# A hybrid block: each HGRN2 head's norm and gate become a task of their own, and the head's outputs use the projections' PSUM banks

## The chip, the cores and the metric

One core of one Trainium2 chip. The metric is the device time of one execution in microseconds (us), lower is better. The engines are TensorE (PE, matmuls; PEld is its weight load), VectorE (DVE), ScalarE (ACT), GpSimd (POOL) and SyncE (SP), which issues most of the DMAs. Matmul results land in PSUM, which has eight banks of 128 x 512 f32.

## What is computed

One layer on 1024 tokens of width 1024: a token-mixing part with three groups of channels, then a mixture of 16 experts. The change is in the readout of the gated linear recurrence (HGRN2), which has four heads of width 128. Cut to what matters:

```python
def hgrn2_inputs(z, lb):
    q, f_fwd, f_bwd, i, g = jnp.split(z, 5, axis=-1)
    q = heads(jax.nn.silu(q)) * (HG_HEAD_DIM ** -0.5)
    for d, f_raw in enumerate((f_fwd, f_bwd)):
        forget = lbd + (1.0 - lbd) * jax.nn.sigmoid(f_raw)
        dirs.append((heads(1.0 - forget), heads(jnp.log(forget))))

def hgrn2_bidir(q, v, dirs, s0_fwd, s0_bwd):
    s_f, o_f = gla_chunk_scan(q, k_f, v, g_f, s0_fwd)
    s_b, o_b = gla_chunk_scan(flip(q), flip(k_b), flip(v), flip(g_b), s0_bwd)
    return s_f, s_b, o_f + flip(o_b)

def hgrn2_readout(o, g, norm_g):
    on = o * lax.rsqrt(jnp.mean(o * o, axis=-1, keepdims=True) + RMS_EPS)
    return on.reshape(B, L, D_HG) * norm_g * jax.nn.silu(g)

y = jnp.concatenate([y_hy, y_hg, y_fn], axis=-1) @ w_out
```

Here o are a head's outputs, `hgrn2_readout` the norm and the gate, and the last line the out-projection, to which every head's gated output is an input.

## The kernel before

The program is written as tasks (Python generators) that a planner, `Weave`, weaves into one order. A task yields what its next piece costs (`T(us)` on PE; `V` or `B` on DVE, ACT and POOL), and the planner always lets the task run next whose piece would start first by its own clocks; among equals the lower rank goes first. `("set", x)` and `("need", x)` order tasks among themselves, and `("spawn", task, rank)` starts one. The order so written is then laid out for each engine by the compiler's scheduler, which also knows when PSUM tiles become free. On the chip each engine works through its own list in that fixed order.

PSUM is split into two pools of four banks: `psc`, from which `self.bank` takes (scores, states, norms), and `psp`, from which `self.pbank` takes (the projections `zps` and, later, the out-projection `mxps`).

In the stretch that the change touches, two tasks run side by side.

* `ins` makes the inputs of the heads (`head_in`): for each of four heads the projections k (forward), k (backward), q and g. One projection holds two of the `psp` banks and is 48 matmuls of 128 x 512 (lines 299 to 301: three products each, since operands are split into a high and a low part, `wh`/`wl`, `hx`). Then ACT and DVE take it out of PSUM. The gate g lies in a buffer of which there is one (`ptp`, `bufs=1`), so from the second head on `head_in` waits for `head{h-1}`, that the head before is done with it, before g is taken out; until then g's projection stays in its two banks. From the third head on, k needs `head{h-2}`. After the four heads comes `open_mix` and the first half of the out-projection, `mix(0)`.
* `outs` runs `fnet`, then the heads one after the other (`heads`, `head`), then `open_moe` and the second half, `mix(1)`.

`head(h)` in order: states of two directions (`kd` on DVE and ACT, `ktps` transposes on PE, `kt` out of PSUM on ACT, `ups` products on PE, `st` updates on DVE); eight levels of scores (`ee` exponentials, `scps` and `strps` products on PE), put together by masked copies (line 1424, then the last four, line 1430, into `scs`); `qd`; the outputs `ops` (lines 1448 to 1450, 24 products, each two records in the trace); the norm (`chan_rstd`, lines 868 to 909: squares `sq` on ACT, their sums `ssps` on PE line 886, twelve small DVE operations from line 584 on for the inverse root `cr`, its split `crh`/`crl`, two diagonal matrices `dg` on DVE and ACT line 897, and `rmsps` on PE line 907, which spreads the factor over the channels); the gate (lines 1460 and 1461 on DVE); and, for heads 0 to 2, a DMA of the result to `ydr`.

I call the stretch from a head's last scores to the next head's first `ups` a seam; there are seam 0 (between heads 0 and 1), 1 and 2, and seam 3 (end of the last head). A period is the time from the first `ops` of a head to the first `ops` of the next.

Of the kernel before, what the change touches and what calls it, by code (L numbers as in the profile page):

```python
# [268 lines left out]
def T(us):  # L269
    return ("pe", us)  # L270


class Kern:
# [889 lines left out]
    def hg_setup(self):  # L1163
# [8 lines left out]
        nc.vector.tensor_copy(self.lvm, m)  # L1172

    def head_in(self, heads):

        nc = self.nc
# [106 lines left out]
    def heads(self):  # L1283
        for h in range(4):
            yield ("need", f"q{h}")
            yield from self.head(h)
            yield ("set", f"head{h}")

    def head(self, h):
        nc, p = self.nc, self.hgp  # L1290
        vec = nc.vector
        hs = slice(h * P, h * P + P)
        r = self.hd[h]
# [40 lines left out]
        for d, (nm, e) in enumerate(zip(nms, (127, 0))):  # L1334
# [9 lines left out]
            for f in range(2):  # L1344
                yield T(0.35)
                ps = self.bank(name="ktps")
# [7 lines left out]
            for f in (0, 1) if d == 0 else (1, 0):  # L1354
                yield T(0.9)
                ps = self.bank(name="ups")
# [17 lines left out]
        for i, f in ((i, f) for i in range(8) for f in range(2)):  # L1374
# [26 lines left out]
            if hh != 16 and f == 0:  # L1401
                ps = self.bank(P, 256, name="strps")
            for c in range(4):
                for n in range(4):
                    a = 32 * n
                    if hh == 16:
                        o = sc[f][a : a + 32, c * P + a : c * P + a + 32]
                    else:
                        o = ps[a : a + 32, (4 * f + c) * 32 : (4 * f + c) * 32 + 32]
# [29 lines left out]
        o = []  # L1439
        yield ("wait", "sc")  # L1440
        yield ("wait", "qd")
        for f in range(2):
            yield T(2.6)
            ps = self.bank(name="ops")
            for c in range(4 * f, 4 * f + 4):
                w = ps[:, (c % 4) * P : (c % 4) * P + P]
                cs = slice(c * P, c * P + P)
                nc.tensor.matmul(w, self.v[:, c, hs], scs[:, cs], start=True, stop=False)
                nc.tensor.matmul(w, st[0][:, c], qd[0][:, cs], start=False, stop=False)
                nc.tensor.matmul(w, st[1][:, c], qd[1][:, cs], start=False, stop=True)  # L1450
            o.append(ps)
        yield ("need", f"g{h}")
        g = r["g"]

        rr = yield from self.chan_rstd(p, [o], P, eps=4 * P * EPS)
        yield V(2.4)
# [4 lines left out]
            vec.tensor_mul(y[:, c], g[:, c], o[f])  # L1461
        if h < 3:
            nc.sync.dma_start(self.ydr[2 + h], y)


    def bcast_row(self, pool, src, name):
# [610 lines left out]
def body(tc, io):  # L2077
    nc = tc.nc
    with ExitStack() as ctx:
# [112 lines left out]


        heads, fn = ExitStack(), ExitStack()
        K.hgs = [pool(f"hg{i}", "right", heads) for i in range(2)]
        K.ptp = pool("pt", "right", heads)
        K.fnp = pool("fnp", "right", fn)
# [123 lines left out]
```

## Time and profile before

| | |
|---|---|
| median of 3 runs | 1416.2 us (1414.52 to 1417.74) |
| the profiled execution's own time | 1413.68 us |
| its span in the profile | 1411.9 us |
| mean granted TensorE clock | 0.954 |
| PE busy | 1248.4 us (88%) |
| PEld busy | 953.9 us (68%) |
| DVE busy | 1080.7 us (77%) |
| ACT busy | 754.3 us (53%) |
| ops(0), first matmul | 575.96 us from the span's start |
| ops(1) | 641.13 |
| ops(2) | 709.16 |
| ops(3) | 787.60 |

Busy shares are means over the whole span, and several stages with different limits lie in it. So the table ends with four marks that cut the heads into three periods: what the change does must be read there. In the views, a "window" row gives busy microseconds and, in brackets, instructions of each engine in a stretch. A "timeline" row gives start, duration, engine, line, operation and tile, and in square brackets the engine's idle time just ahead and what ended it. Matmul records overlap, so a matmul's price is the distance from one start to the next, not its length.

### The profile page before, as it was taken

The numbers are of one execution on the slowest core, as the hardware profiler recorded it, in microseconds if no ns is written. First come the engines' busy times: TensorE is split into PE (matmuls) and PEld (weight loads), VectorE is DVE, ScalarE is ACT, GpSimd is POOL, SyncE is SP. The second block draws the span as 40 slices with busy tenths as digits, with TensorE's granted clock in tenths as the row PEclk, the third lists the DMA queues.
The fourth block names the chain that finished last, engine by engine and source line by source line (L and its number), as shares of the span: only waits on it lengthen the run. The fifth ranks groups of instructions, "written<-read, shape, count | busy, mean of one in ns | idle before, by whom it ended". The sixth has DMA issues, their size and how long they took to land. (4 is left out here: it accounts for less than half of the span.)

```text
span 1411.9 us, 21814 instructions
## 1 busy us (share of the span) xinstructions
PE 1248.4 (88%) x8032; PEld 953.9 (68%) x8032; DVE 1080.7 (77%) x1726; ACT 754.3 (53%) x1043; POOL 117.3 (8%) x131
## 2 busy tenths in 40 slices
PE   5989899999999899999889893899999998989881
PEld 1366678887566687878668772677777776767661
DVE  5567278874222589898988778899999999989965
ACT  2353122334232557666644444677877776777752
POOL 0010010100000000000000000221111012101110
PEclk9699999999999999999989996899999999999995
DMA  7944767727555420101161583899999999899944
GB/s 254 344 139 132 241 207 251 251 100 248 180 164 179 153 62 32 46 32 46 47 209 42 181 318 129 343 343 358 350 336 373 346 367 342 309 322 330 362 133 194
DMA packets 101116, 310.41 MB, mean 220 GB/s; under 512 B 16000, under 2 KB 25792, under 8 KB 100729
## 3 DMA queue, kind: packets, MB, share of 16 engines
q1 hardware_dynamic: 83208, 257.95, 50.0%
q0 software_dynamic: 15472, 48.72, 12.1%
q10 hardware_dynamic: 2304, 2.10, 0.5%
q8 instruction: 70, 1.15, 0.3%
q14 instruction: 62, 0.50, 0.1%
HBM read 274.18 MB, written 43.01 MB: 225 GB/s over the span
## 5 line engine op out<-in xcount | busy, mean ns | idle before, releaser
L293 DVE TENSOR_TENSOR wlo<-raw,whi 128x1024 fp32r<-128x1024 f32 x288 | 339.7, 1218 | 10.9 <-ACT whi L289 6.1
L289 ACT ACTIVATE whi<-raw 128x1024 fp32r<-128x1024 f32 x288 | 300.4, 1058 | 56.8 <-PE gups L301 26.6
L299 PE MATMUL gups<-whi,x 128*128 128x512 f32 x384 | 153.9, 401 | 20.4 <-ACT x L289 17.1
L299 PE MATMUL zps<-hx,wh 128*128 128x512 f32 x384 | 152.9, 398 | 1.2 <-DVE g L1231 1.2
L301 PE MATMUL zps<-hx,wl 128*128 128x512 f32 x384 | 153.0, 399 | 0.0
L300 PE MATMUL zps<-hx,wh 128*128 128x512 f32 x384 | 151.8, 395 | 0.0
L301 PE MATMUL gups<-whi,x 128*128 128x512 f32 x384 | 149.8, 396 | 2.0 <-issue 2.0
L300 PE MATMUL gups<-wlo,x 128*128 128x512 f32 x384 | 151.3, 394 | 0.0
L299 PEld LDWEIGHTS gups<-whi,x 128*128 128x128 f32 x384 | 73.0, 190 | 38.9 <-ACT x L289 20.9
L299 PE MATMUL dnps<-whi,ht 128*128 128x512 f32 x192 | 78.1, 407 | 21.6 <-ACT ht L289 21.6
L300 PEld LDWEIGHTS gups<-wlo,x 128*128 128x128 f32 x384 | 73.1, 190 | 16.9 <-issue 2.1
L300 PEld LDWEIGHTS zps<-hx,wh 128*128 128x128 f32 x384 | 72.5, 189 | 16.7 <-issue 2.9
L299 PEld LDWEIGHTS zps<-hx,wh 128*128 128x128 f32 x384 | 72.5, 189 | 16.2 <-DVE g L1231 1.7
L301 PEld LDWEIGHTS gups<-whi,x 128*128 128x128 f32 x384 | 72.7, 189 | 15.1
L301 PEld LDWEIGHTS zps<-hx,wl 128*128 128x128 f32 x384 | 72.5, 189 | 14.6 <-issue 0.4
L300 PE MATMUL dnps<-wlo,ht 128*128 128x512 f32 x192 | 75.9, 395 | 0.0
L301 PE MATMUL dnps<-whi,ht 128*128 128x512 f32 x192 | 74.9, 415 | 1.0 <-DVE ht L293 0.8
L293 DVE TENSOR_TENSOR wl<-wraw,wh 128x1024 fp32r<-128x1024 f32 x32 | 39.1, 1221 | 39.1 <-ACT wh L289 33.3
L1316 DVE TENSOR_TENSOR ee<-nm 128x1024 f32<-128x1024 f32 x56 | 67.7, 1218 | 0.6 <-PE scps L1396 0.5
L289 ACT ACTIVATE wh<-wraw 128x1024 fp32r<-128x1024 f32 x32 | 33.8, 1057 | 62.6 <-PE zps L300 27.6
L299 PE MATMUL mxps<-woh,yoh 128*128 128x512 f32 x128 | 54.4, 429 | 10.7 <-ACT yoh L289 8.3
L1860 POOL DMA_INDIRECT xg<-h2dr,ix x25 | 28.6, 1144 | 401.0 <-PE gups L301 228.3
(490 smaller groups left out, 2665.2 us busy)
## 6 DMA issues: line engine op xcount, KB each, us to landing
raw<-in_gu_dram SPq DMA_DIRECT2D x192, 512.0 KB, 7.3
raw<-in_dn_dram SPq DMA_DIRECT2D x96, 512.0 KB, 5.8
wraw<-in_win_dram SPq DMA_DIRECT2D x32, 512.0 KB, 4.1
aw<-in_ada_dram SPq DMA_DIRECT2D x32, 512.0 KB, 4.0
aws<-in_ada_dram SPq DMA_DIRECT2D x16, 512.0 KB, 7.6
tabh<-in_fwh_dram POOLq DMA_DIRECT2D x16, 512.0 KB, 5.4
tabl<-in_fwl_dram POOLq DMA_DIRECT2D x16, 512.0 KB, 7.1
xt<-in_x_dram SPq DMA_DIRECT2D x8, 512.0 KB, 4.3
```

The source lines that it names most:

```text
L289: nc.scalar.activation(hi, src, AF.Copy)
L293: nc.vector.tensor_sub(lo, src, hi)
L299: nc.tensor.matmul(out, lh, rh, start=start, stop=False)
L300: nc.tensor.matmul(out, lh, rl, start=False, stop=False)
L301: nc.tensor.matmul(out, ll, rh, start=False, stop=stop)
L1316: vec.tensor_tensor(view(ee, at, *two), view(nms[d], at, *two), view(nms[d], mid, [0, 2], blocks, [0, hh]), op=OP.subtract)
L1860: self.nc.gpsimd.indirect_dma_start(out=self.xg[g], out_offset=None, in_=self.h2dr if src is None else src, in_offset=bass.IndirectOffsetO ...
```

## The change

`ops` is taken from `self.pbank` where it was taken from `self.bank`. What followed `ops` in `head`, the norm and the gate, becomes a task `head_out`, which `head` spawns at its end with rank -8+h, ahead of the others (0 and up) among equals. The mark `head{h}` is set at the end of `head_out` and not by `heads`, and `heads` waits for `head3` at its end. The next head's task thus need not wait for the norm and gate of the one before in the planner. The operations, their sizes and the DMAs are the same.

```diff
     def heads(self):
         for h in range(4):
             yield ("need", f"q{h}")
             yield from self.head(h)
-            yield ("set", f"head{h}")
+        yield ("need", "head3")
...
         yield ("wait", "qd")
         for f in range(2):
             yield T(2.6)
-            ps = self.bank(name="ops")
+            ps = self.pbank(name="ops")
             for c in range(4 * f, 4 * f + 4):
...
             o.append(ps)
+
+        yield ("spawn", self.head_out(h, o), -8 + h)
+
+    def head_out(self, h, o):
+
+        nc, p = self.nc, self.hgp
+        vec = nc.vector
         yield ("need", f"g{h}")
-        g = r["g"]
+        g = self.hd[h]["g"]
 
         rr = yield from self.chan_rstd(p, [o], P, eps=4 * P * EPS)
...
         if h < 3:
             nc.sync.dma_start(self.ydr[2 + h], y)
+        yield ("set", f"head{h}")
```

How the lists of the engines move. First PE in seam 0, before: `strps` are the last scores of head 0, `zps` the projections for the next head, `ops` head 0's outputs.

```order
L1411 MATMUL strps<-ee 32x32 x32
L1411 MATMUL strps<-q,ks 32x32 x32
L300 MATMUL zps<-hx,wh 128x512
...
L1448 MATMUL ops<-scs,v 128x128
L1449 MATMUL ops<-qd,st_4007 128x128
L1450 MATMUL ops<-qd,st_4120 128x128
...
L886 MATMUL ssps<-onesr,sq 128x1 x4
L301 MATMUL zps<-hx,wl 128x512
L299 MATMUL zps<-hx,wh 128x512
```

The same place on PE after the change, from the last scores of head 0 to head 1's first states (`ktps`, `ups`); `lbps` is a small product of the router's setup.

```order
L301 MATMUL zps<-hx,wl 128x512
L1411 MATMUL strps<-ee 32x32 x96
L1411 MATMUL strps<-q,ks 32x32 x32
L1448 MATMUL ops<-scs,v 128x128
L1449 MATMUL ops<-qd,st_4007 128x128
L1450 MATMUL ops<-qd,st_4120 128x128
...
L886 MATMUL ssps<-onesr,sq 128x1 x8
L907 MATMUL rmsps<-dg,onesr 128x512 x4
L1349 MATMUL ktps<-ident,kd 128x128 x8
L1358 MATMUL ups<-v,kt 128x128 x8
L1577 MATMUL lbps<-rw,onesr 128x16 x8
L299 MATMUL zps<-hx,wh 128x512
```

Of the 50 projection matmuls that stood before `ops(0)` behind the same point of the list, and of the 33 between `ops(0)` and head 1's first `ups`, none is left there. In seam 1 there were 21 between the last scores and `ops` and 32 behind them, now none of either; in seam 2 there were 1 and some 13, of the out-projection, now 12 and none. Counted from one head's first `ops` to the next head's, the projection and out-projection matmuls are 171, 164 and 208 before and 192, 192 and 192 after; behind `ops(3)` 175 before and 192 after. The reason is in the pools: `ops` hold two of the four `psp` banks until the gate has read them, and the next head's g, which waits for that same gate, holds the other two.

DVE in seam 0, before: `crl` and `dg` belong to head 0's norm, `kd` and `st` to head 1's states, lines 1460 and 1461 are head 0's gate.

```order
L293 TENSOR_TENSOR crl<-cr_r,crh 128x8
L899 TENSOR_TENSOR dg<-ident,crh 128x1024
L1338 TENSOR_TENSOR kd<-nm_4044 128x1024
L1460 SCALAR_TENSOR_TENSOR z<-z,hgh,rmsps 128x512 x2
L1461 TENSOR_TENSOR z<-z,ops 128x512 x2
L1572 COPY lb<-lbps 128x16
L1338 TENSOR_TENSOR kd<-nm_4155 128x1024
L1366 SCALAR_TENSOR_TENSOR st_4713<-st_4713,eb_4679,ups 128x128
```

And after, where the gate has the lines 1467 and 1468:

```order
L293 TENSOR_TENSOR crl<-cr_r,crh 128x8
L899 TENSOR_TENSOR dg<-ident,crh 128x1024
L1338 TENSOR_TENSOR kd<-nm_4044 128x1024
L1467 SCALAR_TENSOR_TENSOR z<-z,hgh,rmsps 128x512 x2
L1468 TENSOR_TENSOR z<-z,ops 128x512 x2
L1338 TENSOR_TENSOR kd<-nm_4155 128x1024
L1366 SCALAR_TENSOR_TENSOR st_4688<-st_4688,eb_4659,ups 128x128
L1580 COPY lb<-lbps 128x16
L1366 SCALAR_TENSOR_TENSOR st_4688<-st_4688,eb_4659,ups 128x128 x6
L1231 SCALAR_TENSOR_TENSOR g<-g,zps 128x512 x2
```

Head 1's first `kd` stood ahead of head 0's gate already before, and still does; what moved on DVE is that head 1's own g now comes behind the seven updates of the first state.

## Rows read from the trace of the kernel before

**Rows 1.** The three periods in windows: busy us and instructions of each engine.
```profile
core 0: us, PE busy (x) PEld busy (x) DVE busy (x) ACT busy (x) POOL busy (x), PEclk, DMA share, GB/s
575.96:641.13 65.17, 62.35 (x785) 52.18 (x783) 60.47 (x89) 44.14 (x61) 0.00 (x0) 1.00 0.14 45
641.13:709.16 68.03, 59.26 (x760) 48.98 (x761) 61.68 (x89) 42.97 (x60) 0.00 (x0) 0.96 0.17 61
709.16:787.60 78.44, 74.22 (x805) 60.01 (x804) 66.93 (x113) 34.33 (x54) 0.00 (x0) 0.95 0.35 114
```

**Rows 2.** Two windows of 10 us, one in head 0, one in head 3.
```profile
550.00:560.00 10.00, 9.99 (x165) 7.77 (x165) 10.00 (x11) 7.25 (x9) 0.00 (x0) 1.00 0.05 9
...
740.00:750.00 10.00, 10.00 (x72) 8.14 (x70) 6.75 (x15) 1.27 (x2) 0.00 (x0) 1.00 0.18 52
```

**Rows 3.** PE's timeline in seam 0 (columns as told above).
```profile
558.34 0.39 PE L301 MATMUL zps<-hx,wl 128*128 128x512 f32 x1
...
573.23 0.39 PE L301 MATMUL zps<-hx,wl 128*128 128x512 f32 x1
...
575.72 0.40 PE L300 MATMUL zps<-hx,wh 128*128 128x512 f32 x1
575.96 0.38 PE L1448 MATMUL ops<-scs,v 128*128 128x128 f32 x2
...
583.60 0.95 PE L886 MATMUL ssps<-onesr,sq 128*128 128x1 f32 x8
...
589.07 0.85 PE L907 MATMUL rmsps<-dg,onesr 128*128 128x512 f32 x3
...
594.45 2.05 PE L1358 MATMUL ups<-v,kt 128*128 128x128 f32 x16
...
597.04 1.04 PE L1349 MATMUL ktps<-ident,kd 128*128 128x128 f32 x8
```

**Rows 4.** ACT's timeline in seam 0.
```profile
582.17 0.59 ACT L876 ACTIVATE sq<-ops 128x512 f32<-128x512 f32 x1
...
587.29 2.46 ACT L897 ACTIVATE dg<-ident,crl 128x128 fp32r<-128x128 f32 x8 [1.12 <-DVE crl L293]
...
591.05 1.06 ACT L1339 ACTIVATE kd<-kd 128x1024 f32<-128x1024 f32 x1
```

**Rows 5.** DVE's timeline in seam 0.
```profile
584.59 0.17 DVE L584 TENSOR_SCALAR cr_h<-ssps 128x8 f32<-128x8 f32 x1 [0.66 <-PE ssps L886]
...
589.96 0.75 DVE L1460 SCALAR_TENSOR_TENSOR z<-z,hgh,rmsps 128x512 f32<-128x512 f32 x1 [0.44 <-PE rmsps L907]
...
595.65 0.35 DVE L1366 SCALAR_TENSOR_TENSOR st<-st,eb,ups 128x128 f32<-128x128 f32 x1 [1.30 <-PE ups L1358]
```

**Rows 6.** PE's timeline, last scores and first outputs, in seams 1 and 3.
```profile
634.82 0.74 PE L1411 MATMUL strps<-q,ks 128*32 128x32 f32 x62
...
641.13 0.46 PE L1448 MATMUL ops<-scs,v 128*128 128x128 f32 x2 [0.57 <-DVE scs L1430]
...
783.21 0.74 PE L1411 MATMUL strps<-q,ks 128*32 128x32 f32 x62
...
787.60 0.46 PE L1448 MATMUL ops<-scs,v 128*128 128x128 f32 x2
```

**Rows 7.** PE's timeline in seam 2, from the last scores to head 3's transposes.
```profile
701.35 0.74 PE L1411 MATMUL strps<-q,ks 128*32 128x32 f32 x62
708.57 0.79 PE L299 MATMUL mxps<-woh,yoh 128*128 128x512 f32 x1 [6.48 <-ACT yoh L289]
709.16 0.63 PE L1448 MATMUL ops<-scs,v 128*128 128x128 f32 x2
...
714.28 0.42 PE L1448 MATMUL ops<-scs,v 128*128 128x128 f32 x2
...
724.46 2.09 PE L907 MATMUL rmsps<-dg,onesr 128*128 128x512 f32 x4 [0.55 <-DVE dg L899]
726.90 1.59 PE L1349 MATMUL ktps<-ident,kd 128*128 128x128 f32 x8 [0.35 <-DVE g L1460]
```

## The prediction, made before the changed kernel was run

> **What bounds the kernel now.** The page's busy shares (PE 88%, DVE 77%) mix stages, so I first cut the trace into the three periods from one head's first `ops` to the next one's [rows 1]. In the first, 65.17 us long, PE works 62.35 us and DVE 60.47: PE stands idle for 2.8 us only, DVE for 4.7. In the second PE is idle for 8.8 us, DVE for 6.3; in the third for 4.2 and 11.5. Within a period the two take turns: DVE is full in the scores of head 0 while PE is full too, and in head 3 PE stays full while DVE has a third of its time free [rows 2]. PE is full because projection matmuls fill every hole in the heads' own chains. Their pitch is 0.227 us (eleven steps from 573.23 to 575.72) [rows 3], so a projection of 48 takes 10.9 us and four of them, what a period has to hold, 43.6. In the first period 171 of them are 38.8 us; the other 23.5 us of PE's work are scores, states, outputs and norm. So PE's amount of work sets the pace in the first period, with DVE close behind, and the seams are the places where the heads' own chain alone would leave PE idle.
>
> **What the change does to PE's list.** It keeps every operation and DMA, and DVE's list hardly moves: the next head's first `kd` stood ahead of the gate before and still does, so the overlap with the next head's states that the change makes possible in the planner was there already in the list that runs. What moves is the filler. With `ops` in two of the four `psp` banks and the waiting g in the other two, no projection can be laid into the seams. The 50 matmuls ahead of `ops(0)` and the 33 behind it are gone from seam 0, the 21 and 32 from seam 1, the 13 behind `ops(2)` from seam 2. They are done later, when PE has its own work to do. I cost that period by period, each against its own length in the trace.
>
> **The chain in a seam.** From `ops` to the end of the next head's first `ups`, with nothing between: `ops` 5.5 us (575.96 to 581.5); second half of the squares 0.6 [rows 4]; their sums 0.8 and the small DVE operations 2.7 (584.59 until ACT starts on `dg` at 587.29) [rows 3 to 5]; `dg` on ACT 2.5 and the exponential of `kd` behind it 1.1 [rows 4]; transposes, their copy and `ups` 3.3 (593.2, where the transposes begin, to 596.5) [rows 3]. Together 16.5, and one us for some eight hand-overs from engine to engine, which DVE shows as waits of 0.44 to 1.30 where PE's filler came in between [rows 5]: 17.5 us. PE's own part is 5.5 for `ops`, 1.9 for `ssps`, 1.3 for `rmsps`, 1.0 for `ktps` and 2.1 for `ups` [rows 3], 11.8. So PE is idle for about **5.7 us in each seam**; I allow 1 us either way. `rmsps` and the gate run beside the exponential and the transposes and set no end here.
>
> **The masks ahead of `ops`.** After the last scores DVE still has masked copies to make before `ops` can run. PE covered that with filler. From the start of the last scores to `ops` it is 4.4 us in seam 3 (783.21 to 787.60) and 6.3 in seam 1 (634.82 to 641.13) [rows 6]; without the scores themselves, 0.7, that is 3.7 and 5.6. In seam 1 PE will be idle for all of it; I take 3.7, since in seam 1 a weight split was laid in between on DVE, and keep 3.0 and 5.6 as ends. In seam 2, 12 matmuls stay (2.7 us) and leave 1.0. In seam 0 DVE, not PE, leads up to `ops(0)` (full in that stretch [rows 2]), so I leave `ops(0)` at 576 us, cost nothing and expect PE idle instead: its last projection ahead of `ops(0)` will be the one that now starts at 558.34 [rows 3]. If DVE had slack there, `ops(0)` would come earlier, which is in the rivals.
>
> **The sum at full clock.**
> First period: 21 more matmuls, 4.8; the seam, 5.7; the masks, 3.7 less the 0.57 that PE waits there now [rows 6]: +13.6.
> Second: 192 for 164, 6.4; the seam 5.7; masks 1.0 less about 0.6; and less the 6.48 that PE now waits for the out-projection's first operands at 708.57 [rows 7], since projections stand there instead: +6.0.
> Third: 192 for 208, -3.6; the seam 5.7; masks 1.0; less the 4.2 of idle time that the period has now [rows 1] and less the 3.8 that it now pays for the lower clock (worked out below): -4.9.
> Behind `ops(3)`: 17 more, 3.9.
> Sum **18.6**.
>
> **The clock.** After 6.48 us without work PE's matmuls run at 1.2 GHz until 714.28 and at 2.4 behind it [rows 7]; the granted clock of that period is 0.95 [rows 1]. The price is read there: 12 pairs of `ops` take 5.12 us where they would take 2.68 at the later pitch, 2.4 more; `rmsps` 2.09 after a wait against some 1.2 in seam 0, where three of the four take 0.85, and `ktps` 1.59 against 1.04 [rows 3, 7], 1.4 more. Whether the clock falls in the new seams no row shows. Without any fall the cost is 0; with both in all three seams, 11.4. I take `rmsps` and `ktps` in all three (4.2), which stand behind waits just as at 724.46, and the `ops` part once, in seam 0 (2.4), where PE's list has only scores for some 16 us: **6.6**.
>
> The profiled run of 1413.7 us becomes 1413.7 + 18.6 + 6.6 = 1438.9. The median of the runs is 2.5 above that run, so 1416.2 + 25.2 = **1441 us**. The experts behind the mixing do the same work and are moved as a whole.
>
> **Rivals.**
> *DVE is the bound and PE's holes cost nothing; faster.* The place is again the seams: with no filler in front of `ssps`, `rmsps` and `ups`, DVE no longer waits for them (0.66, 0.44 and 1.30 in seam 0 [rows 5]), and the norm and the states come earlier. If DVE set the pace, the first two periods would shrink by up to DVE's idle time in them, 4.7 and 6.3 [rows 1], half of which I give to the seams or all of it: 1405 to 1411 us. It decides if PE has slack left for the displaced matmuls, at least 4.8 us in the first period. Against it: PE has 2.8 there and must lay 53 displaced matmuls (12 us) of seam 1 and 33 of seam 0 outside the seams. For it: PE's busy time is a soft measure.
> The Trainium skill says so as a rule ("Perfetto Trace Analysis", Identifying the Most-Contended Engine): busy share is a fair measure for VectorE, but for TensorE matmul busy time is not, and weight-load busy time is to be used. By that measure the first period has PE at 52.18 of 65.17 (80%) and DVE at 60.47 (93%) [rows 1], and DVE would be the engine to relieve, which gives this rival's 1405 to 1411. What speaks against the rule here is the pitch: with matmuls of 512 columns back to back the weight load is busy 7.77 of 10 us while PE takes no more work [rows 2].
> *The holes close elsewhere; nearly the same.* The change does not do what it says (the overlap was there), and the displaced matmuls fall into time in which PE waits today: 2.8, 8.8 and 4.2 us of idle in the periods [rows 1], against 51 more matmuls behind `ops(0)` (11.6 us) and the seams. If the seams are only half as long as I make them and the clock stays up, 0 to +8: 1416 to 1424 us.
> *The clock falls for whole seams; slower still.* If every `ops` runs at 1.2 GHz throughout, each head pays 4.9 (24 pairs at 0.427 instead of 0.223 [rows 7]), 19.6 for four, and `rmsps` and `ktps` 4.2: 23.8 instead of 6.6. With half to all of that excess: 1450 to 1458 us.
>
> **How the numbers follow.** Forecast (PE paces, seams are holes): 0.75. DVE the bound: 0.10. Holes close elsewhere: 0.10, of which 0.04 within 0.2% (2.8 us, about what a measurement of this kernel can tell from no change). Clock low throughout: 0.05. The forecast's own range: down by 6.6 (clock never falls), 3 (three seams a us shorter) and 0.7 (masks) to 1431; up by 4.8 (`ops` at the lower clock in two more seams), 3 and 1.9 to 1451. To hold the time 8 times in 10 the range goes down into the second rival, 1421 to 1452; what is left out is the faster rival and about half of each of the other two, 0.17. Faster 0.10, same 0.04, slower 0.86.
>
> **What would show it.** In the profile after: no `zps` between the last scores of heads 0 and 1 and the next head's first `ups`; PE idle for some 6 us in each seam behind `ops`, by waits for `sq`, `dg` and `kt`; `ops(0)` at 576, `ops(1)` near 658 (641 before), `ops(2)` near 734 (709), `ops(3)` near 808 (788); a granted clock below 1.00 in the first period. In the periods, DVE idle for more than 4.7 and 6.3 us. It is wrong if `ops(1)` comes at 641 or sooner (DVE paces), or if the seams are filled by work that I did not see; and if the seams are as said but the end moves less, then the out-projection or the experts took it back.

## The result and the profile after

The changed kernel takes 1440.1 us (median, 1437.5 to 1442.4), the kernel before 1417.0 in the runs beside it: a ratio of 1.0165 (95% interval 1.0138 to 1.0191), 20 to 27 us slower. 1441 was forecast. The profiled execution has a span of 1439.8 us (1411.9 before) and a mean granted clock of 0.942 (0.954).

First the windows, cut at the first `ops` of each head as in [rows 1], which has the columns. In the first fence the changed kernel: the stretch ahead of `ops(0)` and the three periods.

```profile
500.00:575.34 75.34, 62.70 (x745) 51.16 (x743) 70.15 (x106) 48.86 (x68) 0.00 (x0) 0.90 0.15 44
575.34:659.24 83.90, 73.34 (x804) 61.27 (x805) 63.24 (x90) 45.06 (x61) 0.00 (x0) 0.91 0.12 39
659.24:735.52 76.28, 69.09 (x788) 57.07 (x788) 56.51 (x83) 40.96 (x57) 0.00 (x0) 0.93 0.05 16
735.52:813.87 78.35, 68.21 (x789) 55.61 (x789) 68.84 (x114) 37.20 (x57) 0.00 (x0) 0.93 0.43 141
```

The same stretch ahead of `ops(0)` in the kernel before:

```profile
500.00:575.96 75.96, 72.62 (x797) 58.84 (x795) 71.18 (x108) 50.14 (x71) 0.00 (x0) 1.00 0.14 44
```

The periods are 83.9, 76.3 and 78.4 us where they were 65.2, 68.0 and 78.4 [rows 1]. PE is idle for 12.6 us ahead of `ops(0)` (3.3 before), and for 10.6, 7.2 and 10.1 in the periods (2.8, 8.8, 4.2). From `ops(3)` to the end of the span it is 625.9 us after and 624.3 before. DVE's work in the three periods is the same in sum (188.6 us, 189.1 before); its idle time grows to 20.7 and 19.8 us in the first two (4.7 and 6.3 before).

PE's timeline in seam 0 of the changed kernel, to be held against [rows 3]:

```profile
557.54 0.76 PE L1411 MATMUL strps<-ee 128*32 128x32 f32 x64
...
559.50 0.40 PE L301 MATMUL zps<-hx,wl 128*128 128x512 f32 x1
561.99 0.75 PE L1411 MATMUL strps<-ee 128*32 128x32 f32 x64 [2.09 <-DVE ee L1382]
567.99 1.08 PE L1411 MATMUL strps<-ee 128*32 128x32 f32 x64 [5.26 <-DVE ee L1382]
570.17 1.08 PE L1411 MATMUL strps<-ee 128*32 128x32 f32 x64 [1.09 <-DVE ee L1382]
...
575.34 0.79 PE L1448 MATMUL ops<-scs,v 128*128 128x128 f32 x2 [3.23 <-DVE scs L1430]
...
580.62 0.56 PE L1448 MATMUL ops<-scs,v 128*128 128x128 f32 x2
...
583.47 1.90 PE L886 MATMUL ssps<-onesr,sq 128*128 128x1 f32 x16
589.36 2.05 PE L907 MATMUL rmsps<-dg,onesr 128*128 128x512 f32 x4 [3.99 <-DVE dg L899]
591.56 1.97 PE L1349 MATMUL ktps<-ident,kd 128*128 128x128 f32 x8 [0.15 <-ACT kd L1339]
593.42 2.61 PE L1358 MATMUL ups<-v,kt 128*128 128x128 f32 x16
595.87 1.86 PE L1577 MATMUL lbps<-rw,onesr 128*128 128x16 f32 x16
597.58 0.48 PE L299 MATMUL zps<-hx,wh 128*128 128x512 f32 x1
```

The last projection matmul is the sixth behind the score level at 557.54, the same one that starts at 558.34 in [rows 3]. Then 38 us pass without one. PE waits for DVE's levels, for the masks, for `dg`, and does the first half of `ops` at the lower clock (twelve pairs in 5.3 us, from 575.34 to 580.62). Over the heads these waits add up as follows (PE's waits from 520 to 880 us: sum, times, longest):

```profile
PE rmsps L907 <- DVE dg L899: 16.4, 4, 7.0
PE strps L1411 <- DVE ee L1382: 10.7, 5, 5.3
PE ops L1448 <- DVE scs L1430: 10.5, 4, 4.6
```

### The profile page after: what moved, and what is told of

Same layout as the page of the kernel before. It is cut to its first block, busy times and chain, and to the rows that moved or that the text cites. A ratio compares the mean times of both kernels' runs of the same rounds, so it can differ in the third digit from the quotient of the medians.

```text
span 1439.8 us, 21803 instructions
## 1 busy us (share of the span) xinstructions
PE 1255.8 (87%) x8032; PEld 961.7 (67%) x8032; DVE 1081.7 (75%) x1726; ACT 755.6 (52%) x1043; POOL 115.6 (8%) x131
## 5 line engine op out<-in xcount | busy, mean ns | idle before, releaser
L299 PEld LDWEIGHTS gups<-whi,x 128*128 128x128 f32 x384 | 72.7, 189 | 34.9 <-ACT x L289 20.9
L301 PEld LDWEIGHTS gups<-whi,x 128*128 128x128 f32 x384 | 72.5, 189 | 17.9 <-issue 3.1
L300 PEld LDWEIGHTS gups<-wlo,x 128*128 128x128 f32 x384 | 72.7, 189 | 14.7
L289 ACT ACTIVATE x<-xtps 128x512 fp32r<-128x512 f32 x48 | 29.9, 624 | 55.7 <-PE xtps L1881 47.9
```

What stands on the lines that cost most here:

```text
L289: nc.scalar.activation(hi, src, AF.Copy)
L299: nc.tensor.matmul(out, lh, rh, start=start, stop=False)
L300: nc.tensor.matmul(out, lh, rl, start=False, stop=False)
L301: nc.tensor.matmul(out, ll, rh, start=False, stop=stop)
```

## The experiments

Marks (the first `ops` of each head) are from one profiled execution of each kernel, and a few us between two marks prove nothing by themselves: head 0's first transposes start at 530.5 us in after_h0 and at 534.0 in after_fill, where the code ahead of them is the same. The last column is the span behind `ops(0)`, the fifth counts the projection and out-projection matmuls behind `ops(0)` in PE's list.

| kernel | median us | ratio to before (95%) | ops(0) | matmuls behind | periods | behind ops(0) |
|---|---|---|---|---|---|---|
| before | 1413 to 1417 | | 576.0 | 718 | 65.2, 68.0, 78.4 | 835.9 |
| changed | 1440.1 | 1.0165 (1.0138 to 1.0191) | 575.3 | 768 | 83.9, 76.3, 78.4 | 864.5 |
| bank_only | 1451.0 | 1.0276 (1.0244 to 1.0308) | 574.5 | 768 | 83.3, 81.9, 81.5 | 872.7 |
| spawn_only | 1409.7 | 0.9952 (0.9932 to 0.9971) | 580.1 | 718 | 64.6, 64.1, 78.2 | 827.9 |
| after_h0 | 1427.0 | 1.0093 (1.0063 to 1.0124) | 573.8 | 768 | 83.1, 65.5, 83.2 | 851.4 |
| after_g2 | 1438.7 | 1.0178 (1.0151 to 1.0205) | 585.7 | 768 | 71.7, 72.7, 80.3 | 851.4 |
| split35 | 1437.2 | 1.0156 (1.0114 to 1.0198) | 587.8 | 768 | 77.3, 73.8, 77.3 | 848.2 |
| spawn35 | 1413.5 | 0.9991 (0.9968 to 1.0013) | 590.5 | 697 | 68.0, 66.5, 71.0 | 825.4 |
| own33 | 1422.4 | 1.0072 (1.0043 to 1.0101) | 583.7 | 707 | 61.4, 71.4, 78.3 | 833.0 |
| spawn_only_g2 | 1416.8 | 1.0027 (1.0004 to 1.0049) | 585.1 | 696 | 65.7, 58.3, 76.6 | 825.4 |
| after_fill | 1438.8 | 1.0170 (1.0137 to 1.0202) | 581.1 | 768 | 80.5, 75.9, 78.6 | 857.4 |
| after_fill2 | 1441.6 | 1.0196 (1.0166 to 1.0226) | 576.9 | 768 | 80.5, 76.0, 78.5 | 861.1 |
| before_pe | 1422.9 | 1.0064 (1.0042 to 1.0087) | 583.5 | 720 | 65.7, 69.1, 84.8 | 839.0 |
| before_dve | 1419.2 | 1.0052 (1.0030 to 1.0073) | 578.5 | 705 | 66.7, 63.5, 84.3 | 837.5 |

### The two halves of the change apart

bank_only, on the kernel before:

```diff
-            ps = self.bank(name="ops")
+            ps = self.pbank(name="ops")
```

> The kernel before with one edit: ops in the projections' banks; norm and gate stay in the head's own task. Bank theory (two psp banks for ops and two for the waiting g leave no bank for filler): its PE list has the same empty seams as the changed kernel (0, 0 and 9 projection matmuls in seam 0; none in seam 1; none in seam 2), so the whole loss: 1434 to 1444 us. Task theory (the norm and gate as a task of their own reorder the work and that is what costs): 1413 to 1421 us.

spawn_only, on the changed kernel:

```diff
-            ps = self.pbank(name="ops")
+            ps = self.bank(name="ops")
```

> The changed kernel with one edit undone: ops back in the banks of scores and states; norm and gate stay a task of their own. Bank theory: the PE list has the filler of the kernel before again (13 and 33 matmuls in seam 0, 20 and 32 in seam 1, against 13 and 33, 21 and 32), so 1413 to 1421 us, no difference that can be measured. Task theory: 1434 to 1444 us.

The bank alone costs more than the whole change: 36 us by the medians, 11 above the changed kernel (16 by the ratios) and above the range that I gave. The task alone is 0.3 to 0.7% faster than the kernel before, outside its range too, if by little, and so **faster than both kernels**. The loss is the bank's, and the task gives some of it back: 11 us or more with the bank, some 7 (4 to 10, by the interval) without.

Without the bank, the task gains 4.0 us in the second period and 3.5 in the third and the stretch behind `ops(3)` together. The second period, first of spawn_only (68.03 us before [rows 1]), then of bank_only (76.28 in the changed kernel):

```profile
644.71:708.78 64.07, 59.25 (x761) 48.61 (x761) 59.36 (x86) 40.95 (x57) 0.00 (x0) 1.00 0.09 33
```

```profile
657.79:739.72 81.93, 70.45 (x788) 58.62 (x788) 60.19 (x87) 43.59 (x60) 0.00 (x0) 0.90 0.14 44
```

spawn_only does the same 59.25 us of PE's work as before (59.26) with 4.8 us of idle time in place of 8.8. In seam 2 of its list six filler matmuls stand ahead of `ops` where one stood, and PE's wait of 6.48 us [rows 7] has gone; a wait of 3.3 us for the masks stands there. With the bank, the changed kernel's second period is 5.7 us shorter than bank_only's, and the lists show 12 matmuls ahead of `ops(2)` with the task and none without.

### One seam only

after_h0, on the changed kernel:

```diff
-            ps = self.pbank(name="ops")
+            ps = (self.pbank if h == 0 else self.bank)(name="ops")
```

> The changed kernel with ops in the projections' banks for head 0 only. Bank theory, summed like the prediction: first period 44 more matmuls (10.0 us), the empty seam 5.7, the clock 3.8, together +19.5; second +0.5 for 2 matmuls and -6.5 for the wait at the out-projection's start, which projections now cover; third 12 fewer, -2.7; behind ops(3) 16 more, +3.6: +14, about 1431 us (1425 to 1437). If each seam costs a third of the whole: 1424 us. Task theory: 1440 us, since the task is there for all heads.

1427.0 us, at the low side of what the sum gave (1431) and clear of the task theory (1440). From a third for each seam (1424) the time alone does not tell it apart: the interval is 1424 to 1432 us. The marks do. The first period grows by 17.9 us (19.5 expected). Against spawn_only, from which it differs in head 0's `ops` alone, it is 17 us slower, and the changed kernel 30: seam 0 costs more than half. The later steps of that sum were less good: the second period shrank by 2.5 us where 6.0 was expected, the third grew by 4.8 us where -2.7 was expected, and the stretch behind `ops(3)` shrank by 4.7 where +3.6 was expected. The last two together are +0.1 where +0.9 was expected, so there the sum only missed where `ops(3)` falls.

### Why the filler is gone: banks or order

after_g2, on the changed kernel (cut to its core; g is rounded to bf16 so that two buffers fit):

```diff
-                    t = x = (self.hgs[h % 2] if kind == "q" else self.ptp).tile([P, L], F32, name=kind, bufs=1)
+                    if kind == "q":
+                        t = x = self.hgs[h % 2].tile([P, L], F32, name="q", bufs=1)
+                    else:
+                        t = x = self.ptp.tile([P, L], BF, name="g", bufs=2)
...
-            if kind == "g" and h:
-                yield ("need", f"head{h - 1}")
+            if kind == "g" and h > 1:
+                yield ("need", f"head{h - 2}")
...
-        y = g if h < 3 else self.y3
+        y = self.hd[h]["q"] if h < 3 else self.y3
```

> The changed kernel with two buffers for the gate g, so that g leaves its two PSUM banks without waiting for the head before; to make room g is rounded to bf16, and the gated result is written into the head's q buffer. ops stay in the projections' banks. Theory that it is the two together, ops and a g that waits, that empty the seams: the list has 28, 34 and 13 filler matmuls behind ops again, though still none ahead of ops(0); the 51 matmuls moved behind ops(0) are in part laid into the seams: 1417 to 1428 us. Rival, that ops in the projections' banks cost by themselves, whatever g does: 1434 to 1444 us.

The time says that it changes nothing, 1438.7 us. The marks say more: behind `ops(0)` it is 13 us faster than the changed kernel, as expected, but `ops(0)` comes 10 us later. Its filler behind `ops` is back and its filler ahead of `ops(0)` is not; there PE works 62.85 of 85.65 us. DVE took q and g of head 1 out of PSUM in that stretch and was full from 550 to 580 us. So I took the banks out of the question in another way, with more of them.

split35, on the changed kernel:

```diff
-        K.psc = mps.enter_context(tc.tile_pool(name="psc", bufs=4, space=PS))
-        K.psp = mps.enter_context(tc.tile_pool(name="psp", bufs=4, space=PS))
+        K.psc = mps.enter_context(tc.tile_pool(name="psc", bufs=3, space=PS))
+        K.psp = mps.enter_context(tc.tile_pool(name="psp", bufs=5, space=PS))
```

> The changed kernel with PSUM cut 3 to 5 in place of 4 to 4: ops stay in the projections' pool, which has one bank more (the pool of scores and states one less). Its PE list has filler behind ops again (27, 27 and 7 projection matmuls up to the next head's first ups) but still none ahead of ops in seams 0 and 1; the counts between outputs stay 192, 192, 192. Theory that two things empty the seams, the shared pool's order ahead of ops and the lack of a free bank behind them: about the price of the empty seams behind ops comes back, some 6 us and 1.4 of clock in each of seams 0 and 1, less in seam 2, while the 51 matmuls that moved behind ops(0) stay there: 1420 to 1428 us. Theory of the prediction (only the lack of a free bank): all of it comes back, 1412 to 1419 us. That filler is not what counts: 1436 to 1444.

spawn35, the same cut with `ops` among scores and states:

```diff
-            ps = self.pbank(name="ops")
+            ps = self.bank(name="ops")
```

> As split35 (PSUM cut 3 to 5, norm and gate a task of their own), but ops among scores and states: the two differ in nothing but the pool that ops come from. The list has filler ahead of ops (16, 19, 9) and behind (46, 41, 20), and 697 projection matmuls behind ops(0) where split35 has 768. Theory of the shared pool's order (a projection that is written behind ops cannot be laid ahead of them, so 0.227 us for each of 71 displaced matmuls, 16 us): 14 to 20 us faster than split35's 1437, 1417 to 1423 us. If split35 is slow because of the cut 3 to 5: about as slow as split35, 1432 us or more.

split35 again gains behind `ops(0)` (16 us against the changed kernel) and loses it ahead (`ops(0)` 12.5 us later, 8 of it already at head 0's first scores), 1437.2 us in all and outside the 1420 to 1428 that I expected. By itself that could be the fault of the cut 3 to 5. spawn35 excludes it: 1413.5 us with that cut, 24 us faster than split35 (more than the 14 to 20 expected), and the two differ in the pool of `ops` alone. The windows ahead of `ops(0)` and of the first period, split35 first:

```profile
500.00:587.84 87.84, 69.28 (x793) 56.63 (x791) 82.63 (x123) 55.48 (x77) 0.00 (x0) 0.91 0.14 44
587.84:665.18 77.34, 69.43 (x804) 57.53 (x804) 59.06 (x86) 43.14 (x60) 0.00 (x0) 0.96 0.10 35
```

```profile
500.00:590.45 90.45, 88.34 (x883) 71.45 (x882) 84.92 (x126) 62.19 (x88) 0.00 (x0) 1.00 0.15 49
590.45:658.42 67.97, 66.79 (x801) 55.35 (x801) 60.26 (x88) 44.61 (x62) 0.00 (x0) 1.00 0.09 32
```

Both reach `ops(0)` at nearly the same time, with DVE nearly full in both (83 of 88, 85 of 90 us). But in spawn35 PE has worked 88.3 us by then, in split35 69.3. The 71 matmuls that split35 still has to do at 0.227 us are 16 of the 23 us by which the two differ behind `ops(0)` (848.2 and 825.4). What PE waits for from 500 to 830 us, in split35 and then in spawn35:

```profile
PE strps L1411 <- DVE ee L1382: 14.9, 6, 5.7
PE ops L1448 <- DVE scs L1430: 11.5, 3, 5.6
```

```profile
PE strps L1411 <- DVE ee L1382: 7.4, 3, 3.9
...
PE ops L1448 <- DVE scs L1430: 1.7, 3, 0.9
```

A fifth bank does not fill these waits as long as `ops` come from the same pool. The lists of the changed kernel, bank_only, after_g2 and split35, all of which take `ops(0)` from the projections' pool, have no projection between the last scores and `ops(0)` and 768 behind it, with four banks or five, with g waiting or not.

own33, on the changed kernel, gives `ops` two banks of their own:

```diff
-        K.psc = mps.enter_context(tc.tile_pool(name="psc", bufs=4, space=PS))
-        K.psp = mps.enter_context(tc.tile_pool(name="psp", bufs=4, space=PS))
+        K.psc = mps.enter_context(tc.tile_pool(name="psc", bufs=3, space=PS))
+        K.psp = mps.enter_context(tc.tile_pool(name="psp", bufs=3, space=PS))
+        K.pso = mps.enter_context(tc.tile_pool(name="pso", bufs=2, space=PS))
...
-            ps = self.pbank(name="ops")
+            ps = self.pso.tile([P, 512], F32, tag="bank", name="ops")[:P, :512]
```

> The changed kernel with PSUM cut 3, 3 and 2: ops get two banks of their own, projections keep three, scores and states three. Its PE list has filler both ahead of ops (16, 17, 12) and behind (23, 27, 4). Theory of the shared pool's order: as good as the kernel before or the one with ops back among scores and states, 1406 to 1417 us, though the projections have fewer banks than in the changed kernel. Theory that the number of free projection banks counts: no better than the changed kernel, 1430 us or more.

1422.4 us lies between what the two theories gave, 18 us better than the changed kernel though the projections have a bank less, and 6 to 14 us worse than the kernel before. The list has the filler ahead of `ops` again (16, 17 and 12), and behind `ops(0)` it is no slower than the kernel before (833.0 us for 835.9, in an execution that was the fastest of its eight). What the three banks cost shows in a wait that neither the kernel before nor the changed one has at that size, for the copies out of a projection's banks (from 500 to 900 us):

```profile
PE zps L299 <- ACT nm L1259: 5.9, 4, 2.6
```

The sharing can be priced by itself: own33 and split35 both leave three banks to scores and states and five to the projections and `ops` together, and giving `ops` two of the five for themselves is worth 15 us by the medians; the two intervals are just clear of each other. With all five for the projections and `ops` among the scores (spawn35) it is 9 us less again. So both count, the pool's order more. That the scheduler hands out a pool's tiles in the order in which they are written, and so cannot lay a later projection ahead of `ops`, fits the lists of seam 0 in all these kernels; the runs show the effect in time, not the rule itself.

spawn_only_g2 is spawn_only with the edit of after_g2.

> ops among scores and states, norm and gate a task of their own, and two buffers for the gate g (rounded to bf16, the gated result written into the head's q buffer), so that g never waits in PSUM for the head before. If the wait of g still costs anything once ops are out of the projections' banks: below the kernel with one g buffer, 1400 to 1408 us. If not: 1407 to 1413 us.

1416.8 us, outside both. A second gate buffer makes spawn_only slower, not faster, and its runs scatter from 1412 to 1426. The edit also rounds g and makes the loaded g wait in a buffer of head 1's, so I can't say which of its parts costs. It does not speak for the waiting g as a cause.

### What the clock costs

after_fill, on the changed kernel; `mk` is a mask in bf16:

```diff
+    def idle(self, n):
+        ps = self.bank(name="dummy")
+        for _ in range(n):
+            self.nc.tensor.matmul(ps, self.mk[:, :P], self.mk[:, :512], start=True, stop=True)
...
+            if h == 0 and f == 1 and hh in (4, 2):
+                self.idle(16 if hh == 2 else 8)
+            if h < 2 and f == 1 and hh == 0:
+                self.idle(12)
...
+        if fill:
+            self.idle(14)
         yield V(3.9, 1.8)
```

> The changed kernel with idle matmuls (bf16, 512 columns, read by nobody) in the holes of the seams, so that PE is busy there: 8 and 16 between the last score levels of head 0, 12 ahead of ops in seams 0 and 1, 14 between the sums of squares and rmsps in seams 0 to 2. The order of the other work is kept. Clock theory: the lower clock in the changed kernel's trace costs 0.9 us on head 0's last scores, 2.6 and 1.3 on ops in seams 0 and 1, 0.8 to 1 each on rmsps and ktps in three seams, some 1 on ups, together about 10; with PE kept busy it comes back: 1428 to 1434 us. If the clock is no cost of its own (the lower clock only where PE waits anyway): 1437 to 1443 us.

I had put 16 idle matmuls into a hole of 1.1 us; they put off `ops(0)`, and the time stayed at 1438.8. after_fill2 puts them right:

```diff
-            if h == 0 and f == 1 and hh in (4, 2):
-                self.idle(16 if hh == 2 else 8)
+            if h == 0 and f == 1 and hh in (8, 4, 2):
+                self.idle({8: 6, 4: 16, 2: 3}[hh])
             if h < 2 and f == 1 and hh == 0:
-                self.idle(12)
+                self.idle(10)
```

> The idle matmuls of after_fill, in better measure: 6, 16 and 3 between head 0's last score levels (holes of 2.1, 5.3 and 1.1 us in the changed kernel's trace) and 10 ahead of ops, so that none stands in the way. In after_fill the 16 stood in the hole of 1.1 us and put off ops(0). From ops(0) to ops(1) after_fill took 80.5 us, the changed kernel 83.9; in the second period it gained 0.4 only. Clock theory, corrected: 2.6 for ops(0) and 0.9 for ktps in the first period, 1 to 2 in each of the others: 1432 to 1436 us, from ops(0) to the end 5 to 8 us less than the 864.5 of the changed kernel. The prediction's sum would give back 6.6, 1433 us. If the clock costs nothing: 1438 to 1443.

PE's timeline in seam 0 of after_fill2 (its lines 909, 1356 and 1365 are `rmsps`, `ktps` and `ups`):

```profile
576.90 0.49 PE L1459 MATMUL ops<-scs,v 128*128 128x128 f32 x2 [1.54 <-DVE scs L1441]
...
582.36 0.95 PE L886 MATMUL ssps<-onesr,sq 128*128 128x1 f32 x8
...
588.75 0.93 PE L909 MATMUL rmsps<-dg,onesr 128*128 128x512 f32 x3 [1.59 <-DVE dg L901]
...
590.95 1.09 PE L1356 MATMUL ktps<-ident,kd 128*128 128x128 f32 x8 [0.44 <-ACT kd L1346]
592.36 2.05 PE L1365 MATMUL ups<-v,kt 128*128 128x128 f32 x16
594.25 1.86 PE L1588 MATMUL lbps<-rw,onesr 128*128 128x16 f32 x16
```

The clock stays at its upper level in this seam, `ops` take 5.5 us for 8.1, `rmsps` and `ktps` are back at their short times, and from `ops(0)` to the matmuls behind `ups` (`lbps`) it is 17.4 us in place of 20.5. The first period shrinks by 3.4 us to 80.5. The second does not (76.0 for 76.3), although `rmsps` and `ktps` became shorter in seam 1 as well. `rmsps` runs beside the exponential on ACT, and `ktps` waits for that exponential: in seam 0 it starts 2.20 us behind `rmsps` in both kernels. `ops(1)` did not become shorter, 7.1 us in both (5.4 before). In seam 2 the idle matmuls did not keep the clock up; `rmsps` and `ktps` take as long as in the changed kernel:

```profile
748.61 2.04 PE L909 MATMUL rmsps<-dg,onesr 128*128 128x512 f32 x4 [4.99 <-DVE dg L901]
750.74 1.97 PE L1356 MATMUL ktps<-ident,kd 128*128 128x128 f32 x8
```

So the third period (78.5 for 78.4) tells nothing about the clock. The idle matmuls also cost something: three of them stand between the two halves of `ssps` in seams 0 and 1 and put off the norm by some 0.5 us. In the median no gain is left (1441.6, expected 1432 to 1436). What is shown is that the clock costs some 3 us in seam 0, and that the longer `rmsps` is not paid. What it costs in `ops(1)` and in seam 2 stays open.

### Who sets the pace

before_pe, on the kernel before, with `idle` as above:

```diff
+            if f == 1 and hh == 8:
+                self.idle(22)
             if hh == 16:
                 yield B(0, 0.5)
```

> The kernel before with 22 idle matmuls (bf16, 512 columns, read by nobody) in the scores of each of the four heads, about 5 us of PE's time per head, 20 in all. If PE's work paces the heads: 15 to 20 us slower, 1430 to 1435. If DVE paces them: the matmuls go into PE's slack, 0 to 5 us slower.

before_dve, on the kernel before:

```diff
+            if f == 1 and hh == 8:
+                for _ in range(4):
+                    vec.tensor_tensor(self.mk, self.mk, self.mk, op=OP.mult)
             if hh == 16:
                 yield B(0, 0.5)
```

> The kernel before with four idle DVE operations (128x1024 bf16, a mask times itself) in the scores of each of the four heads, 16 in all, at 0.3 to 1.2 us each by their size; the trace will give it. If PE paces the heads: 0 to a third of their sum. If DVE does: their whole sum, 5 to 19 us.

What was added, from the groups by line (count, then busy us and mean ns), first on PE, then on DVE:

```profile
L1292 PE MATMUL dummy<-mk 128*128 128x512 bf16 x88 | 19.7, 380 | 0.0
```

```profile
L1414 DVE TENSOR_TENSOR mk<-mk 128x1024 bf16<-128x1024 bf16 x16 | 10.9, 682 | 0.0
```

19.7 us more on PE cost 6 to 12 us (0.42 to 0.87%), 10.9 us more on DVE cost 4 to 10. Neither theory has it: 0.3 to 0.6 of PE's extra work is paid and 0.4 to 0.9 of DVE's, two ranges that overlap. Where PE's went, in before_pe ahead of `ops(0)` and in the second and third period:

```profile
500.00:583.51 83.51, 80.25 (x817) 63.24 (x815) 76.52 (x112) 51.98 (x72) 0.00 (x0) 0.96 0.15 46
...
649.20:718.34 69.14, 67.13 (x797) 53.58 (x798) 59.92 (x86) 42.45 (x60) 0.00 (x0) 1.00 0.07 24
718.34:803.12 84.78, 77.26 (x828) 60.27 (x828) 68.72 (x115) 34.72 (x55) 0.00 (x0) 0.98 0.41 135
```

The second period takes 7.9 us more of PE's work than in [rows 1] and is 1.1 us longer, because its 8.8 us of idle time filled up. The third is 6.3 us longer, of which the stretch behind `ops(3)` gives 4.9 back. Most is paid ahead of `ops(0)`, which comes 7.5 us later, 5.7 of it between head 0's first scores and `ops(0)`: there the idle matmuls of head 0 stand (4.9 us), and PE had only 3.3 us of idle time and still has it. So in this execution extra work on PE was paid where PE was full and hardly where it waits. That the two engines bound the heads in turn fits this, but is not shown. The list moved in both runs (in the first two periods 157 and 179 projection matmuls in before_pe and 187 and 136 in before_dve, for 171 and 164 before), so the numbers by stage are less certain than the times.

## Why the prediction was right, and where it was not

The sum was 18.6 us at full clock and 6.6 for the clock, 25.2; the spans differ by 27.9, the medians by 23. By stage, clock included, the measured change is 1.3 us above the forecast in the first period, 0.9 in the second and 3.4 in the third, and 2.3 below it behind `ops(3)`.

* **PE's list and the holes: right.** No projection between the last scores and the next `ups`, `ops(0)` unmoved (575.3), `ops(1)` at 659 (658 forecast), `ops(2)` at 736 (734). The first period grew by 18.7 us (13.6 and 3.8 of the clock forecast), the second by 8.3 (6.0 and 1.4).
* **The chain of a seam: right.** 17.5 us from `ops` to the end of `ups` was summed from the rows; after_fill2, at full clock and with only idle matmuls and one projection matmul laid into seam 0, shows 17.4. PE's idle time in the changed kernel is 4.1 us in seams 0 and 1, not 5.7, since PE's own work took longer at the lower clock; nearly all of it is the wait for `dg` (4.0), and the waits for `sq` and `kt` that I expected hardly show (0.3 us, for `sq` in seam 2).
* **The clock: the mechanism right, the size open.** `ops(0)` at the lower clock cost 2.6 us (2.4 forecast), and after_fill2 got it back. Of the 4.2 for `rmsps` and `ktps` in three seams, the part of `rmsps` was wrong: I had written myself that it sets no end there, and then priced it. For `ops(1)` I had put nothing into the sum, only into the range, and it took 7.1 us where it took 5.4 before. What all of it cost together was not measured: after_fill2 shows some 3 us in seam 0 and nothing in the kernel's time, but it left `ops(1)` and seam 2 at the lower clock.
* **The third period: mis-sized the other way.** -4.9 was forecast, with 1.4 for the clock, and it did not change (78.35). In seam 2 PE waits 7.0 us for `dg`, not 4.0. DVE's timeline shows why, from the norm's first small operation to `dg`:

```profile
743.45 0.16 DVE L584 TENSOR_SCALAR cr_h<-ssps 128x8 f32<-128x8 f32 x1
743.52 0.68 DVE L293 TENSOR_TENSOR wol<-woraw,woh 128x512 fp32r<-128x512 f32 x1
744.12 0.17 DVE L585 TENSOR_SCALAR cr_r<-cr_h 128x8 int32<-128x8 int32 x1
...
748.31 0.17 DVE L293 TENSOR_TENSOR crl<-cr_r,crh 128x8 fp32r<-128x8 f32 x1
748.39 0.68 DVE L1488 TENSOR_TENSOR woraw<-woraw,gate 128x512 f32<-128x512 f32 x1
748.99 1.22 DVE L899 TENSOR_TENSOR dg<-ident,crh 128x1024 fp32r<-128x1024 f32 x1
```

The out-projection's operations (splits, and weights times gate) stand among the small operations, each 0.68 us, and the chain takes 5.0 us from its first operation to `crl` where it takes 2.7 in seam 0. I had carried seam 0's price over to a seam where DVE's list is another. The stretch behind `ops(3)` grew by 1.6 and not by 3.9, which takes most of this error back. In after_h0 and before_pe, too, what the third period gained the stretch behind `ops(3)` lost (4.8 and 4.7, 6.3 and 4.9), so the two are better read together: +0.4 forecast, +1.5 measured. That the total is off by a few us only is in part luck.
* **Why the filler could not be laid there: half right.** I named the banks, two for `ops` and two for the waiting g. With a fifth bank or with g not waiting, filler came back behind `ops` and the stretch behind `ops(0)` became 13 to 16 us shorter, so that is a part. But ahead of `ops` it did not come back, and the time stayed. What empties the place ahead in seams 0 and 1 is that `ops` share a pool with the projections at all (split35 against spawn35 and own33). In seam 2, 12 out-projection matmuls stayed ahead, as the list had shown.
* **"PE's amount of work sets the pace": too strong.** It held for this change, which took away PE's cover and moved 50 matmuls from a stretch where DVE leads to periods that PE had to lengthen. As a general statement about the heads it is wrong: a good part of PE's extra work went into idle time (0.3 to 0.6 of it was paid), and 0.4 to 0.9 of DVE's was paid.
* **The rivals.** DVE as the only bound would have shrunk the periods; they grew by 18.7 and 8.3. Holes that close elsewhere gave 1416 to 1424; PE's idle time grew in the first and third period instead. The clock stayed low for parts of `ops` in seams 0 and 1, not throughout. The Trainium skill ("Perfetto Trace Analysis", Identifying the Most-Contended Engine) does not judge TensorE by its matmul busy time but by weight-load busy time and the share of peak arithmetic, and by weight-load busy time DVE was the engine to relieve. before_dve agrees in part, 10.9 us more on it cost 4 to 10, but more work on PE cost time as well, and the change took nothing off DVE. The 7.77 of 10 us that I held against that rule came from a window with 128 score matmuls in it. In the kernel before, 21 matmuls of 512 columns back to back, and nothing else, show the same:

```profile
562.00:566.60 4.60, 4.60 (x21) 3.77 (x21) 4.60 (x6) 4.32 (x5) 0.00 (x0) 1.00 0.00 0
```

The weight load is busy for 82% there with PE full, so the 80% of the first period did not leave PE a fifth of its time.

## What to carry to other kernels

Before moving a tile from one PSUM pool to another, look at what else comes from that pool: on the engine's list, work that filled another engine's waits may no longer be laid ahead of the moved tile, and here a fifth bank did not bring it back. Price such a change by counting the filler on either side of each waiting place and by summing the bare chain there, and take each place's chain from its own rows, since another place can have other work in its engine's list. And try the halves of a change apart: here the task alone was faster than both kernels (1409.7 us), and the bank alone was the slowest of all.

## What the runs showed of the hardware that I had not expected

Where PE waits for other engines anyway, the lower granted clock cost less here than its rows suggest. In the changed kernel `ktps` is 0.9 us and `rmsps` about 0.8 us longer in seams 0 to 2. after_fill2 took this away in seams 0 and 1, yet only the first period became shorter, by 3.4 us, of which 2.6 are `ops(0)`; the idle matmuls themselves cost some 0.5 us in each of the two seams. With idle matmuls in the holes of seam 0, PE waited for 1.54 us ahead of `ops(0)`, which ran at 2.4 GHz throughout. In seam 1 of the same kernel it waited for 3.31 us ahead of `ops(1)`: the first products start 0.23 us apart, then products of one kind start 1.28 us apart, at 1.2 GHz, and 0.67 apart behind 661.81:

```profile
657.40 0.49 PE L1459 MATMUL ops<-scs,v 128*128 128x128 f32 x2 [3.31 <-DVE scs L1441]
657.72 0.39 PE L1460 MATMUL ops<-qd,st 128*128 128x128 f32 x2
657.95 0.54 PE L1461 MATMUL ops<-qd,st 128*128 128x128 f32 x2
658.28 0.64 PE L1459 MATMUL ops<-scs,v 128*128 128x128 f32 x2
...
659.56 0.63 PE L1459 MATMUL ops<-scs,v 128*128 128x128 f32 x2
...
661.81 0.39 PE L1459 MATMUL ops<-scs,v 128*128 128x128 f32 x2
...
662.48 0.39 PE L1459 MATMUL ops<-scs,v 128*128 128x128 f32 x2
```
